# Up projection of a ConvFFN with its weights on the array: channels by tokens instead of tokens by channels

## The chip, the cores and the metric

The kernel runs on one core of a Trainium2 chip. A core has a matrix engine (PE; the loading of its stationary operand has a row of its own, PEld), a vector engine (DVE), a scalar engine (ACT), GpSimd (POOL) and a queue that issues transfers (SP). Matrix products read SBUF and write PSUM, which here is eight banks of 128 by 512 float32. Times are device microseconds of one execution. The program before took 1526.14 us, the median of three runs (1524.74 to 1528.38).

## The reference

One layer of a decoder trunk for 256 tokens of width 2048: a combined projection, two attentions, a gated merge, an output projection, and then a gated feed-forward block with a causal convolution of width 3 over the tokens. Only that last block changes:

```
def conv_ffn(h, w_up, conv_w, conv_b, w_down):
    a, b = jnp.split(h @ w_up, 2, axis=-1)          # h (256, 2048), w_up (2048, 2 x 5632)
    ap = jnp.pad(a, ((0, 0), (CONV_WIDTH - 1, 0), (0, 0)))
    c = conv_b
    for j in range(CONV_WIDTH):
        c = c + conv_w[j] * ap[:, j:j + S]
    return (jax.nn.gelu(c, approximate=True) * b) @ w_down
```

`h` is the RMS-normed residual `x2`. The kernel multiplies the norm's gain into `x2` beforehand; the norm's factor `r` is one number per token, so it can be applied after the product.

## The kernel before

**Products in three parts.** Every float32 operand is held as a rounded high part and the rest as a low part. A product is the sum of high x high, high x low and low x high, three matmuls into one PSUM bank (`mm3`, lines 149 to 151). For weights the split is made on the fly: `wchunk` brings 512 KB of weights (two k-tiles of 128 rows by 512 columns) into a buffer `raw`, ACT copies it rounded to `whi` (L124), DVE subtracts to get `wlo` (L125). There are five `whi`, five `wlo` and three `raw` buffers.

**`gemm`.** For a block of 512 output columns it goes through the k-tiles. The activations are the stationary operand (128 tokens by 128 k), the weights move (512 columns). There are two token tiles, so one k-tile costs six matmuls of 512 columns, and the result stands as tokens by channels in two PSUM banks, one for each token tile.

**The up projection.** `ffn_up(c)` runs for c = 0 to 10, each for 512 channels of the activation half `a` and then the same 512 of the gate half `b`: two `gemm` of eight chunks each. The convolution runs over tokens, so it wants channels by tokens. ACT evacuates each half scaled by `r` (tiles `f`, L866). `conv_cols` then takes 128 channels at a time: four PE transposes (two halves, two token tiles; L844) put `a` and `b` side by side in a PSUM tile `fT`; ACT and DVE do the convolution, the tanh form of the gelu and the product with `b` (L848 to L856); the result is split into `gh` and `gl`, the stationary operand of the down projection.

**What sets the order.** The source hands work to a list of steps: `at(t, f)` puts `f` at a step, and `gemm` calls `tick()` after each chunk. `conv_cols` for the four channel tiles of one c stands at steps 1, 3, 5 and 7 of the next c. A scheduler then sets the order of each engine's queue, and each engine works its queue strictly in that order. The names in the queues carry a running number (`whi_8553`).

**The tiles of activations.** `slot` makes the 16 high and 16 low tiles of each of two sets (`a`, `b`), each 512 numbers wide and holding two k-tiles of 256 tokens. A slot is 520 numbers long (2080 bytes), so that successive slots start at successive multiples of 32 bytes, and `whi`, `wlo` are 1032 numbers long for the same reason.

**The first c** differs: its first `gemm` runs the second token tile's products at the end (`split`), while the residual of that tile is still being computed, and `r` (`rf`) comes from a sum of squares and a Newton iteration on DVE.

Of the kernel before, what the change touches and what calls it, by code (L numbers as in the profile page):

```python
# [23 lines left out]
KT = D // P
# [5 lines left out]
DFF = 5632  # L30
# [11 lines left out]
def trunk_layer(ctx, tc, x, g_mix_pre, g_mix_post, g_ffn_pre, g_ffn_post, w_in, g_q, w_q, g_kv, w_kv,  # L42
                sinks, rel, wo_a, wo_b, w_out, w_up, conv_w, conv_b, w_down, rope_tab, strip_sel, out):
    nc = tc.nc
    vec, act, pe, pool = nc.vector, nc.scalar, nc.tensor, nc.gpsimd
# [6 lines left out]
    pacc = ctx.enter_context(tc.tile_pool(name="pacc", bufs=4, space=PS))  # L52
    pss = ctx.enter_context(tc.tile_pool(name="pss", bufs=2, space=PS))
    pst = ctx.enter_context(tc.tile_pool(name="pst", bufs=2, space=PS))
    dram = ctx.enter_context(tc.tile_pool(name="dram", bufs=1, space=bass.MemoryType.DRAM))
    base = ctx.enter_context(tc.tile_pool(name="base", bufs=1))
    ring = ctx.enter_context(tc.tile_pool(name="ring", bufs=RING))

    def sb(pl, shape, name, dt=F32, tag=None, bufs=None):
        return pl.tile(shape, dt, name=name, tag=tag or name, **({"bufs": bufs} if bufs else {}))  # L60


    ident = sb(base, [P, P], "ident")
# [27 lines left out]


    def slot(name, p, part):
        o = 4 if part == "l" else 0
        return sb(base, [P, 512 + 8], f"{name}{part}{p}", F32R)[:, o:o + 512]

    slot_a = lambda p, part: slot("a", p, part)
    slot_b = lambda p, part: slot("b", p, part)

    def pair_view(tiles):  # L100
        return lambda k: tiles[k // 2][:, (k % 2) * 256:(k % 2) * 256 + 256]
# [4 lines left out]
    def wchunk(src, shape, own=None, rawp=None):  # L106
        i = cnt[0]
        cnt[0] += 1
        n = int(np.prod(shape))
        raw = rawp.tile([P, 1024], F32, name=f"raw{i}", tag="xraw") if rawp else \  # L110
            ring.tile([P, 1024], F32, name=f"raw{i}", tag="raw", bufs=RAW)
        dst = raw[:, :n]
        if len(shape) == 2:
            dst = dst.rearrange("p (a b) -> p a b", a=shape[0])
        elif len(shape) == 3:
            dst = dst.rearrange("p (a b c) -> p a b c", a=shape[0], b=shape[1])
        if len(shape) == 3:
            for k in range(shape[0]):
                nc.sync.dma_start(dst[:, k], src[:, k])
        else:  # L120
            nc.sync.dma_start(dst, src)
        hi, lo = ((own or ring).tile([P, 1024 + (0 if own else 8)], F32R, name=f"w{part}{i}", tag="w" + part)[:, 0:1024]
                  for part in ("hi", "lo"))
        act.copy(hi[:, :n], raw[:, :n])  # L124
        vec.tensor_tensor(lo[:, :n], raw[:, :n], hi[:, :n].bitcast(F32), op=ALU.subtract)  # L125
        return hi, lo
# [3 lines left out]
    now = [0]  # L130

    def at(t, *fs):
        steps[max(t, now[0])].extend(fs)

    def tick():
        for f in steps.pop(now[0], ()):
            f()
        now[0] += 1
# [14 lines left out]
    def gemm(xh, xl, w, k0, nk, c0, n, split=False, pre=None, extra=None):  # L153

        kc = 1024 // n if n in (256, 512) else 2
        acc = new_acc("g")
        todo = []
        cuts = [0, 1, 2] + list(range(4, nk + 1, 2)) if pre else list(range(0, nk, kc)) + [nk]
        for ci, (k, ke) in enumerate(zip(cuts[:-1], cuts[1:])):
            kk = ke - k  # L160
            src = w[(k0 + k) * P:(k0 + k + kk) * P, c0:c0 + n].rearrange("(a p) n -> p a n", p=P)
            if pre and ci == 0:
                pre(k, ke)
            hi, lo = wchunk(src, [kk, n], *(extra or {}).get(ci, ()))
            if pre and ke < nk:
                pre(ke, cuts[ci + 2])
            for j in range(kk):
                kt = k + j
                wh, wl = hi[:, j * n:(j + 1) * n], lo[:, j * n:(j + 1) * n]
                for t in range(NT):  # L170
                    def go(kt=kt, t=t, wh=wh, wl=wl):
                        mm3(acc[t][:, :n], xh(k0 + kt)[:, t * P:(t + 1) * P],
                            xl(k0 + kt)[:, t * P:(t + 1) * P], wh, wl, kt == 0, kt == nk - 1)
                    if split and t == 1:
                        todo.append(go)
                    else:
# [26 lines left out]
    def split_to(hi, lo, src, scale=None):  # L203

        if scale is None:
            act.copy(hi, src)  # L206
            vec.tensor_tensor(lo, src, hi.bitcast(F32), op=ALU.subtract)
        else:
            act.activation(hi, src, AF.Copy, scale=scale)
            vec.scalar_tensor_tensor(lo, src, scale, hi.bitcast(F32), op0=ALU.mult, op1=ALU.subtract)  # L210
# [124 lines left out]
    for g in range(4):  # L335
        at(2 + g, lambda g=g: swa_k(g))

    oth = [slot_b(p, "h") for p in range(8)]
    otl = [slot_b(p, "l") for p in range(8)]
    OH, OL = pair_view(oth), pair_view(otl)  # L340
# [434 lines left out]

    x2h = [slot_b(p, "h") for p in range(8)]
    x2l = [slot_b(p, "l") for p in range(8)]
    HH, HL = pair_view(x2h), pair_view(x2l)
    ssh = [sb(p3, [P, 4], f"ssh{t}") for t in range(NT)]
    rf = [None, None]  # L780

# [20 lines left out]
    def x2_norm(t):  # L802
        for j in range(4):
            act.activation(jk(f"xj{t}_{j}"), x2[t][j], AF.Square, accum_out=ssh[t][:, j:j + 1])
        v = sb(p3, [P, 1], f"vh{t}")
        vec.tensor_reduce(v, ssh[t], axis=AX.X, op=ALU.add)
        vec.tensor_scalar(v, v, 1.0 / D, EPS, op0=ALU.mult, op1=ALU.add)
        r = rsqrt(v, 1, f"rf{t}", p3)
        r2 = sb(p3, [P, 1], f"rfh{t}")
        vec.tensor_scalar(r2, r, 0.5, None, op0=ALU.mult)  # L810
        rf[t] = (r, r2)

    for b in range(4):
        c0, n = W_BLOCKS[b]
# [20 lines left out]
    gT, dsum = [[], []], []  # L835
    GH, GL = pair_view(gT[0]), pair_view(gT[1])

    def conv_cols(sa, k, i, slot):

        w0, w1, w2, cb_ = (cvT[:, 44 * q + k:44 * q + k + 1] for q in range(4))  # L840
        pt = pst.tile([P, 512], F32, name=f"fT{k}", tag="t")
        for q in range(2):
            for t in range(NT):
                pe.transpose(pt[:, q * 256 + t * P:q * 256 + (t + 1) * P], sa[t][q][:, i * P:(i + 1) * P], ident)  # L844
        a, b = pt[:, 0:256], pt[:, 256:512]
        cc = sb(p6, [P, 256], f"cc{k}", tag="cc", bufs=3)
        uu = sb(p6, [P, 256], f"uu{k}", tag="uu", bufs=3)
        act.activation(cc, a, AF.Identity, scale=w2, bias=cb_)  # L848
        vec.scalar_tensor_tensor(cc[:, 1:256], a[:, 0:255], w1, cc[:, 1:256], op0=ALU.mult, op1=ALU.add)
        vec.scalar_tensor_tensor(cc[:, 2:256], a[:, 0:254], w0, cc[:, 2:256], op0=ALU.mult, op1=ALU.add)  # L850
        act.activation(uu, cc, AF.Square)
        vec.tensor_scalar(uu, uu, 0.044715, 1.0, op0=ALU.mult, op1=ALU.add)
        vec.tensor_tensor(uu, uu, cc, op=ALU.mult)
        act.activation(uu, uu, AF.Tanh, scale=GELU_C)
        vec.scalar_tensor_tensor(uu, uu, 1.0, cc, op0=ALU.add, op1=ALU.mult)
        vec.tensor_tensor(uu, uu, b, op=ALU.mult)  # L856
        split_to(GH(slot), GL(slot), uu)

    def ffn_up(c, slot0, first=False):

        sa = [[None, None], [None, None]]

        def evac(acc, q):
            for t in range(NT):
                a = sb(p6, [P, 512], f"f{q}_{c}_{t}", tag="f" + "ab"[q], bufs=4)
                act.activation(a, acc[t], AF.Copy, scale=rf[t][q][:, 0:1])  # L866
                sa[t][q] = a

        acc, todo = gemm(HH, HL, w_up, 0, KT, 512 * c, 512, split=first, extra=first_extra if first else None)
        for f in todo:  # L870
            f()
        if first:
            x2_norm(0)
            x2_norm(1)
        evac(acc, 0)
        if first:
            drain()
            es8.close()
            esx.close()
            es7, p7 = open_pool("p7")  # L880
            for q, part in enumerate("hl"):
                gT[q][:] = [slot_a(i, part) if i < 8 else sb(p7, [P, 512], f"g{part}{i}", F32R) for i in range(12)]
            dsum[:] = [[sb(p7, [P, 512], f"ds{t}_{j}") for j in range(4)] for t in range(NT)]
        acc, _ = gemm(HH, HL, w_up, 0, KT, DFF + 512 * c, 512)
        evac(acc, 1)
        for i in range(4):
            at(now[0] + 1 + 2 * i, lambda i=i: conv_cols(sa, 4 * c + i, i, slot0 + i))
        return es7 if first else None

    es7 = ffn_up(0, 0, first=True)  # L890
# [109 lines left out]
```

## Time and profile before

| | |
|---|---|
| median of three runs | 1526.14 us |
| profiled execution: span | 1523.6 us |
| PE / PEld busy | 99% / 82% of the span |
| DVE / ACT busy | 62% / 52% |
| granted clock of PE, mean | 0.998 |
| transfers | 285 MB, 187 GB/s |

The profile shows one execution. Its own time is given as the span, 1523.6 us from the first to the last instruction; the median of the timed runs is 2.5 us longer, and that difference is taken as what lies around the span. A matmul's row shows its duration from start to end, but matmuls overlap: what one costs is the distance between the starts of two neighbours.

### The profile page before, as it was taken

What the parts mean: (1) busy time and instruction counts of PE and PEld (TensorE: products, weight loads), DVE (VectorE), ACT (ScalarE), POOL (GpSimd) and SP (SyncE); (2) the same over time, 40 slices, a digit from 0 to 9 for tenths busy, and PEclk for the clock granted to TensorE, in tenths of its full rate; (3) what the DMA queues carried; (4) which work ended last, traced back from release to release, by engine and by line L of the source; (5) the groups of instructions that cost most, each with busy time, mean ns of one, the idle gap of its engine ahead of it and who ended that gap; (6) DMA issues with size and microseconds to landing.
All of it is one profiled execution on the core that took longest, in us unless ns stands there. A gap on an engine that the chain in (4) does not pass through costs nothing.

```text
span 1523.6 us, 20149 instructions
## 1 busy us (share of the span) xinstructions
PE 1508.2 (99%) x7347; PEld 1246.6 (82%) x7347; DVE 940.2 (62%) x1607; ACT 799.1 (52%) x1289; POOL 66.8 (4%) x114
## 2 busy tenths in 40 slices
PE   9999999999999999999999999999999999999997
PEld 7888888888899887888888888888888888888887
DVE  5688884444677664655766666666544466666755
ACT  6588874434555553444655545555434455555542
POOL 2122200000000002000000000000000000000000
PEclk9999999999999999999999999999999999999999
DMA  7776666666655658765656666665566666665553
GB/s 236 214 177 166 156 180 188 202 207 201 187 153 153 175 163 298 243 211 186 189 184 179 187 183 181 181 180 181 191 191 186 189 180 180 181 190 181 178 193 113
DMA packets 160803, 285.46 MB, mean 187 GB/s; under 512 B 18419, under 2 KB 33893, under 8 KB 160448
## 3 DMA queue, kind: packets, MB, share of 16 engines
q1 hardware_dynamic: 154736, 264.81, 57.0%
q0 software_dynamic: 5968, 19.36, 5.0%
q8 instruction: 58, 0.95, 0.3%
q14 instruction: 41, 0.34, 0.1%
HBM read 277.79 MB, written 6.34 MB: 186 GB/s over the span
## 4 chain that ended last, share of the span: by engine, by line
PE 93%; DVE 2%; DMA 2%; ACT 2%; issue 1%; SPq 0%; DVEq 0%; ACTq 0%
PE accg L149 28%; PE accg L151 28%; PE accg L150 28%; DMA raw<-in_w_in_dram 1%; PE fT L844 1%; PE mpo L685 1%; DMA raw<-in_w_o_mla_dram 1%; DVE wlo L125 1%; PE ms L651 1%; ACT whi L124 1%; PE qn L616 0%; PE qn L614 0%; PE qn L615 0%; ACT p L411 0%; PE pt L369 0%
## 5 line engine op out<-in xcount | busy, mean ns | idle before, releaser
L125 DVE TENSOR_TENSOR wlo<-raw,whi 128x1024 fp32r<-128x1024 f32 (+2 forms) x501 | 608.8, 1216 | 506.4 <-ACT whi L124 505.7
L124 ACT CAST whi<-raw 128x1024 fp32r<-128x1024 f32 (+2 forms) x501 | 521.5, 1042 | 611.7 <-PE accg L151 514.3
L149 PE MATMUL accg<-whi,bh 128*128 128x512 f32 x960 | 382.3, 398 | 0.0
L151 PE MATMUL accg<-whi,bl 128*128 128x512 f32 x960 | 378.5, 394 | 0.0
L150 PE MATMUL accg<-wlo,bh 128*128 128x512 f32 x960 | 378.1, 394 | 0.0
L149 PE MATMUL accg<-whi,ah 128*128 128x512 f32 (+2 forms) x896 | 347.8, 389 | 0.0
L150 PE MATMUL accg<-wlo,ah 128*128 128x512 f32 (+2 forms) x896 | 344.6, 385 | 0.1
L151 PE MATMUL accg<-whi,al 128*128 128x512 f32 (+2 forms) x896 | 344.0, 384 | 0.0
L151 PEld LDWEIGHTS accg<-whi,bl 128*128 128x128 f32 x960 | 180.2, 188 | 42.6
L150 PEld LDWEIGHTS accg<-wlo,bh 128*128 128x128 f32 x960 | 180.5, 188 | 40.4
L149 PEld LDWEIGHTS accg<-whi,bh 128*128 128x128 f32 x960 | 180.4, 188 | 40.2
L151 PEld LDWEIGHTS accg<-whi,al 128*128 128x128 f32 x896 | 168.6, 188 | 35.0
L150 PEld LDWEIGHTS accg<-wlo,ah 128*128 128x128 f32 x896 | 168.8, 188 | 32.8 <-DVE wlo L125 0.8
L149 PEld LDWEIGHTS accg<-whi,ah 128*128 128x128 f32 x896 | 168.7, 189 | 31.6 <-ACT whi L124 0.2
L149 PE MATMUL accg<-whi,gh 128*128 128x512 f32 (+1 forms) x104 | 39.7, 382 | 0.0
L150 PE MATMUL accg<-wlo,gh 128*128 128x512 f32 (+1 forms) x104 | 39.1, 376 | 0.0
L151 PE MATMUL accg<-whi,gl 128*128 128x512 f32 (+1 forms) x104 | 38.7, 376 | 0.0
L411 ACT ACTIVATE p<-p,nm 128x128 f32<-128x128 f32 x64 | 28.4, 445 | 5.8 <-DVE nm L402 5.8
L844 PEld LDWEIGHTS fT<-ident,f 128*128 128x128 f32 x176 | 21.9, 140 | 6.0
L844 PE MATMUL fT<-ident,f 128*128 128x128 f32 x176 | 26.3, 272 | 0.0
L848 ACT ACTIVATE cc<-fT,cvT 128x256 f32<-128x256 f32 x44 | 24.3, 552 | 0.0
L149 PEld LDWEIGHTS accg<-whi,gh 128*128 128x128 f32 x104 | 19.5, 188 | 4.4 <-ACT gh L206 0.8
(304 smaller groups left out, 1284.9 us busy)
## 6 DMA issues: line engine op xcount, KB each, us to landing
raw<-in_ffn_w_up_dram SPq DMA_DIRECT2D x176, 512.0 KB, 3.9
raw<-in_w_in_dram SPq DMA_DIRECT2D x111, 512.0 KB, 4.3
raw<-in_ffn_w_down_dram SPq DMA_DIRECT2D x88, 512.0 KB, 3.7
raw<-in_w_o_swa_dram SPq DMA_DIRECT2D x32, 512.0 KB, 4.2
raw<-in_w_o_mla_dram SPq DMA_DIRECT2D x32, 512.0 KB, 4.8
raw<-in_w_out_dram SPq DMA_DIRECT2D x32, 512.0 KB, 4.1
raw<-in_mla_w_q_up_dram SPq DMA_DIRECT2D x48, 128.0 KB, 2.7
bias<-strip POOLq DMA_DIRECT2D x16, 256.0 KB, 3.9
```

What stands on the lines that cost most here:

```text
L124: act.copy(hi[:, :n], raw[:, :n])
L125: vec.tensor_tensor(lo[:, :n], raw[:, :n], hi[:, :n].bitcast(F32), op=ALU.subtract)
L149: pe.matmul(o, ah, bh, start=start, stop=False)
L150: pe.matmul(o, ah, bl, start=False, stop=False)
L151: pe.matmul(o, al, bh, start=False, stop=stop)
L411: act.activation(pb[:, i, a:b], pb[:, i, a:b], AF.Exp, bias=st["nm"][:, i, t:t + 1], accum_out=st["sm"][:, i, t:t + 1])
L651: pe.matmul(o, w, v_, start=n == 0, stop=False)
L685: pe.matmul(o, w(t), p_[:, c], start=n == 0, stop=n == 5)
L844: pe.transpose(pt[:, q * 256 + t * P:q * 256 + (t + 1) * P], sa[t][q][:, i * P:(i + 1) * P], ident)
L848: act.activation(cc, a, AF.Identity, scale=w2, bias=cb_)
```

## The change

- **`gemm_t`** is new and computes the up projection, all of it except the `a` half of c = 0. The weights are the stationary operand (128 k by 128 channels), the tokens move. The tokens' high and low parts of one k-tile now lie side by side in one slot of 512 columns (`HS`). For each of four channel tiles, `whi` meets the 512 columns (high and low tokens at once), and `wlo` meets the 256 columns of the high tokens, added to the first half of the same bank. A k-tile of 512 channels is four matmuls of 512 columns and four of 256. Four banks (`pacc`) hold the `a` half, the other four (`pss`, `pst`) the `b` half.
- **The result is already channels by tokens**, so the transposes `fT` go, but for the two of each channel tile in c = 0. In their place ACT copies the low half of the bank to SBUF and DVE adds the high half (`join`), for `a` and for `b`.
- **The factor `r`** can no longer be a per-partition scale. `x2_rows` makes a tile `rfrow` with `r` along the columns (two transposes, once), and DVE multiplies by it, once before the convolution and once after the gelu.
- **The steps:** the convolution of `a` now runs in steps 0 to 3 of the `b` half (`conv_next`), the product with `b` in steps 0 to 3 of the next c (`conv_b`).
- **Lengths:** slots and ring buffers lose their extra 8 numbers, and two pads put the slots and the ring's buffers all at 96 bytes modulo 256.

```
     def slot(name, p, part):
-        o = 4 if part == "l" else 0
-        return sb(base, [P, 512 + 8], f"{name}{part}{p}", F32R)[:, o:o + 512]
+        return sb(base, [P, 512], f"{name}{part}{p}", F32R)
...
+    sb(base, [P, 56], "pad_a")
...
+    def gemm_t(xs, w, nk, c0, acc):
+        for k in range(0, nk, 2):
+            src = w[k * P:(k + 2) * P, c0:c0 + 512].rearrange("(a p) n -> p a n", p=P)
+            hi, lo = wchunk(src, [2, 512])
+            for j in range(2):
+                for i in range(4):
+                    c = j * 512 + i * P
+                    pe.matmul(acc[i], hi[:, c:c + P], xs(k + j), start=k + j == 0, stop=False)
+            for j in range(2):
+                for i in range(4):
+                    c = j * 512 + i * P
+                    pe.matmul(acc[i][:, 0:256], lo[:, c:c + P], xs(k + j)[:, 0:256], start=False, stop=k + j == nk - 1)
+            tick()
...
+    def join(acc, name):
+        a = sb(p6, [P, 512], name, tag="fa", bufs=4)[:, 0:256]
+        act.copy(a, acc[:, 256:512])
+        vec.tensor_tensor(a, a, acc[:, 0:256], op=ALU.add)
+        return a
+
+    def conv_next(acc, k, gs):
+        a = join(acc, f"ca{k}")
+        vec.tensor_tensor(a, a, rfrow[0], op=ALU.mult)
+        conv_a(a, k, gs)
+
+    def conv_b(acc, k, g, slot):
+        b = join(acc, f"cb{k}")
+        vec.scalar_tensor_tensor(g, g, 0.5, b, op0=ALU.mult, op1=ALU.mult)
+        split_to(GH(slot), GL(slot), g)
...
-        acc, _ = gemm(HH, HL, w_up, 0, KT, DFF + 512 * c, 512)
-        evac(acc, 1)
+        else:
+            acc = [pacc.tile([P, 512], F32, name=f"acca{c}_{i}", tag="acc") for i in range(4)]
+            gemm_t(HS, w_up, KT, 512 * c, acc)
+            for i in range(4):
+                at(now[0] + i, lambda i=i: conv_next(acc[i], 4 * c + i, gs))
+        acb = [(pss, pst)[i // 2].tile([P, 512], F32, name=f"accb{c}_{i}", tag="st"[i // 2]) for i in range(4)]
+        gemm_t(HS, w_up, KT, DFF + 512 * c, acb)
         for i in range(4):
-            at(now[0] + 1 + 2 * i, lambda i=i: conv_cols(sa, 4 * c + i, i, slot0 + i))
+            at(now[0] + i, lambda i=i: conv_b(acb[i], 4 * c + i, gg[i], slot0 + i))
```

Two places show how the queues move. The first is PE's queue in the up projection for c = 2. Before, four transposes stand between two chunks of a `gemm` (`accg` is its PSUM tile, `bh` and `bl` are the tokens' high and low parts):

```order
L151 MATMUL accg_0_8172<-whi_8194,bl_6638 128x512
L149 MATMUL accg_1_8173<-whi_8194,bh_6630 128x512
L150 MATMUL accg_1_8173<-wlo_8195,bh_6630 128x512
L151 MATMUL accg_1_8173<-whi_8194,bl_6638 128x512
L844 MATMUL fT_8210<-ident,f_1_0_8018 128x128
L844 MATMUL fT_8210<-ident,f_1_1_8020 128x128
L844 MATMUL fT_8210<-ident,f_1_0_8168 128x128
L844 MATMUL fT_8210<-ident,f_1_1_8170 128x128
L149 MATMUL accg_0_8172<-whi_8230,bh_6631 128x512
```

Now the chunks follow each other with nothing between; this is the end of an `a` half and the first chunk of the `b` half:

```order
L193 MATMUL acca_3_8346<-bl_6646,wlo_8528 128x256
L189 MATMUL accb_0_8547<-bh_6631,whi_8553 128x512
L189 MATMUL accb_1_8548<-bh_6631,whi_8553 128x512
L189 MATMUL accb_2_8549<-bh_6631,whi_8553 128x512
L189 MATMUL accb_3_8550<-bh_6631,whi_8553 128x512
L189 MATMUL accb_0_8547<-bh_6632,whi_8553 128x512
L189 MATMUL accb_1_8548<-bh_6632,whi_8553 128x512
L189 MATMUL accb_2_8549<-bh_6632,whi_8553 128x512
L189 MATMUL accb_3_8550<-bh_6632,whi_8553 128x512
L193 MATMUL accb_0_8547<-bh_6631,wlo_8554 128x256
L193 MATMUL accb_1_8548<-bh_6631,wlo_8554 128x256
```

The transposes are gone, and six matmuls of 512 columns for a k-tile have become four of 512 and four of 256, first all with `whi`, then all with `wlo`.

The second place is DVE's queue. Before, the work of one channel tile is spread over the chunks, with never more than eight other instructions between two `wlo`:

```order
L125 TENSOR_TENSOR wlo_8339<-raw_8336,whi_8338 128x1024
L849 SCALAR_TENSOR_TENSOR cc_8215<-fT_8210,cvT,cc_8215 128x255
L850 SCALAR_TENSOR_TENSOR cc_8215<-fT_8210,cvT,cc_8215 128x254
L125 TENSOR_TENSOR wlo_8357<-raw_8354,whi_8356 128x1024
L852 TENSOR_SCALAR uu_8216<-uu_8216 128x256
L853 TENSOR_TENSOR uu_8216<-uu_8216,cc_8215 128x256
L125 TENSOR_TENSOR wlo_8399<-raw_8396,whi_8398 128x1024
```

Now 22 instructions stand between the fifth and the sixth `wlo` of a `b` half, in every c from 1 to 10. The first ones and the last ones of the 22 for c = 2 (`ca` is the joined `a` of a channel tile, `gg` the gelu's result):

```order
L125 TENSOR_TENSOR wlo_8702<-raw_8699,whi_8701 128x1024
L887 TENSOR_TENSOR ca_8573<-ca_8573,acca_0_8343 128x256
L887 TENSOR_TENSOR ca_8610<-ca_8610,acca_1_8344 128x256
L892 TENSOR_TENSOR ca_8573<-ca_8573,rfrow 128x256
L892 TENSOR_TENSOR ca_8610<-ca_8610,rfrow 128x256
L887 TENSOR_TENSOR ca_8647<-ca_8647,acca_2_8345 128x256
L887 TENSOR_TENSOR ca_8684<-ca_8684,acca_3_8346 128x256
L870 SCALAR_TENSOR_TENSOR cc_8577<-ca_8573,cvT,cc_8577 128x255
```

```order
L876 SCALAR_TENSOR_TENSOR gg_0_8341<-uu_8578,cc_8577 128x256
L874 TENSOR_TENSOR uu_8615<-uu_8615,cc_8614 128x256
L877 TENSOR_TENSOR gg_0_8341<-gg_0_8341,rfrow 128x256
L873 TENSOR_SCALAR uu_8652<-uu_8652 128x256
L892 TENSOR_TENSOR ca_8684<-ca_8684,rfrow 128x256
L874 TENSOR_TENSOR uu_8652<-uu_8652,cc_8651 128x256
L125 TENSOR_TENSOR wlo_8724<-raw_8721,whi_8723 128x1024
```

The convolution of four channel tiles has become one block on DVE, with the tiles' steps interleaved, and the next `wlo` stands behind it. It comes to 22 instructions ahead of the sixth `wlo` and 10 more spread over the next four.

More of the change, by code (lines that the diff above doesn't have):

```diff
@@ L121, in wchunk @@
             nc.sync.dma_start(dst, src)
-        hi, lo = ((own or ring).tile([P, 1024 + (0 if own else 8)], F32R, name=f"w{part}{i}", tag="w" + part)[:, 0:1024]
+        hi, lo = ((own or ring).tile([P, 1024], F32R, name=f"w{part}{i}", tag="w" + part)
                   for part in ("hi", "lo"))
@@ L336, in trunk_layer @@
         at(2 + g, lambda g=g: swa_k(g))
+    sb(base, [P, 8], "pad_b")
     oth = [slot_b(p, "h") for p in range(8)]
@@ L777, in trunk_layer @@
     x2l = [slot_b(p, "l") for p in range(8)]
-    HH, HL = pair_view(x2h), pair_view(x2l)
+    HS = lambda k: (x2h + x2l)[k]
+    HH, HL = (lambda k: HS(k)[:, 0:256]), (lambda k: HS(k)[:, 256:512])
     ssh = [sb(p3, [P, 4], f"ssh{t}") for t in range(NT)]
@@ L808, in x2_norm, with x2_rows @@
         r = rsqrt(v, 1, f"rf{t}", p3)
-        r2 = sb(p3, [P, 1], f"rfh{t}")
-        vec.tensor_scalar(r2, r, 0.5, None, op0=ALU.mult)
-        rf[t] = (r, r2)
+        rf[t] = r
+    def x2_rows():
+        pr = pst.tile([P, 512], F32, name="rfT", tag="t")
+        for t in range(NT):
+            rb = sb(p6, [P, P], f"rfb{t}", tag="uu", bufs=3)
+            vec.tensor_copy(rb, rf[t][:, 0:1].to_broadcast([P, P]))
+            pe.transpose(pr[:, t * P:(t + 1) * P], rb, ident)
+        row = sb(p3, [P, 256], "rfrow")
+        act.copy(row, pr[:, 0:256])
+        return row
     for b in range(4):
@@ L836, in trunk_layer, with conv_a @@
     GH, GL = pair_view(gT[0]), pair_view(gT[1])
-    def conv_cols(sa, k, i, slot):
+    def conv_a(a, k, gs):
         w0, w1, w2, cb_ = (cvT[:, 44 * q + k:44 * q + k + 1] for q in range(4))
[L841 to L845, printed above, removed]
         cc = sb(p6, [P, 256], f"cc{k}", tag="cc", bufs=3)
         uu = sb(p6, [P, 256], f"uu{k}", tag="uu", bufs=3)
+        gg = gs[(k % 4) // 2][:, (k % 2) * 256:(k % 2) * 256 + 256]
         act.activation(cc, a, AF.Identity, scale=w2, bias=cb_)
@@ L854, in conv_cols, with conv_first @@
         act.activation(uu, uu, AF.Tanh, scale=GELU_C)
-        vec.scalar_tensor_tensor(uu, uu, 1.0, cc, op0=ALU.add, op1=ALU.mult)
-        vec.tensor_tensor(uu, uu, b, op=ALU.mult)
-        split_to(GH(slot), GL(slot), uu)
-    def ffn_up(c, slot0, first=False):
[L861 to L871, printed above, removed]
+        vec.scalar_tensor_tensor(gg, uu, 1.0, cc, op0=ALU.add, op1=ALU.mult)
+        vec.tensor_tensor(gg, gg, rfrow[0], op=ALU.mult)
+    def conv_first(sa, k, i, gs):
+        pt = pacc.tile([P, 512], F32, name=f"fT{k}", tag="acc")
+        for t in range(NT):
+            pe.transpose(pt[:, t * P:(t + 1) * P], sa[t][:, i * P:(i + 1) * P], ident)
+        conv_a(pt[:, 0:256], k, gs)
+    def join(acc, name):
[11 more added lines that the diff above has]
+        split_to(GH(slot), GL(slot), g)
+    rfrow = []
+    def ffn_up(c, slot0, first=False):
+        gs = [sb(p6, [P, 512], f"gg{c}_{i}", tag="fb", bufs=4) for i in range(2)]
+        gg = [gs[i // 2][:, (i % 2) * 256:(i % 2) * 256 + 256] for i in range(4)]
         if first:
+            acc, todo = gemm(HH, HL, w_up, 0, KT, 512 * c, 512, split=True, extra=first_extra)
+            for f in todo:
+                f()
             x2_norm(0)
             x2_norm(1)
-        evac(acc, 0)
-        if first:
+            sa = []
+            for t in range(NT):
+                a = sb(p6, [P, 512], f"fa{t}", tag="fa", bufs=4)
+                act.activation(a, acc[t], AF.Copy, scale=rf[t][:, 0:1])
+                sa.append(a)
+            rfrow.append(x2_rows())
             drain()
@@ L883, in ffn_up @@
             dsum[:] = [[sb(p7, [P, 512], f"ds{t}_{j}") for j in range(4)] for t in range(NT)]
-        acc, _ = gemm(HH, HL, w_up, 0, KT, DFF + 512 * c, 512)
-        evac(acc, 1)
+            for i in range(4):
+                at(now[0] + 1 + i, lambda i=i: conv_first(sa, 4 * c + i, i, gs))
+        else:
+            acc = [pacc.tile([P, 512], F32, name=f"acca{c}_{i}", tag="acc") for i in range(4)]
+            gemm_t(HS, w_up, KT, 512 * c, acc)
+            for i in range(4):
+                at(now[0] + i, lambda i=i: conv_next(acc[i], 4 * c + i, gs))
+        acb = [(pss, pst)[i // 2].tile([P, 512], F32, name=f"accb{c}_{i}", tag="st"[i // 2]) for i in range(4)]
+        gemm_t(HS, w_up, KT, DFF + 512 * c, acb)
         for i in range(4):
-            at(now[0] + 1 + 2 * i, lambda i=i: conv_cols(sa, 4 * c + i, i, slot0 + i))
+            at(now[0] + i, lambda i=i: conv_b(acb[i], 4 * c + i, gg[i], slot0 + i))
         return es7 if first else None
```

## The prediction

> **What bounds the kernel now.** I read the page's busy times first, then the chain of waits, then the list of who waited for whom on PE, and last the order of time around one group of transposes.
>
> ```profile
> span 1523.6 us, 20149 instructions
> PE 1508.2 (99%) x7347; PEld 1246.6 (82%) x7347; DVE 940.2 (62%) x1607; ACT 799.1 (52%) x1289; POOL 66.8 (4%) x114
> PE 93%; DVE 2%; DMA 2%; ACT 2%; issue 1%; SPq 0%; DVEq 0%; ACTq 0%
> PE warm L73 <- DVE ident_b L68: 2.0, 1, 2.0
> PE ckT L489 <- DVE ckl L210: 1.3, 1, 1.3
> ```
>
> PE carries 93% of the chain, and its two longest waits on another engine sum to 3.3 us, both far ahead of the feed-forward block. So in that block time is PE's instruction count times the distance of their starts, and nothing else, as long as the weights arrive in time. The distances, in order of time, first around four transposes of c = 1, then in `qn`, an earlier projection that already works the way the change does (weights stationary, 256 token columns moving, a new weight load for each matmul):
>
> ```profile
> 861.44 0.39 PE L151 MATMUL accg<-whi,bl 128*128 128x512 f32 x1
> 861.67 0.60 PE L844 MATMUL fT<-ident,f 128*128 128x128 f32 x4
> 862.02 0.48 PE L149 MATMUL accg<-whi,bh 128*128 128x512 f32 x1
> 862.34 0.39 PE L150 MATMUL accg<-wlo,bh 128*128 128x512 f32 x1
> ...
> 865.11 0.39 PE L150 MATMUL accg<-wlo,bh 128*128 128x512 f32 x1
> 379.27 0.28 PE L614 MATMUL qn<-cqh,whi 128*128 128x256 f32 x1
> ...
> 381.63 0.28 PE L616 MATMUL qn<-cqh,wlo 128*128 128x256 f32 x1
> L844 PE MATMUL fT<-ident,f 128*128 128x128 f32 x176 | 26.3, 272 | 0.0
> ```
>
> A matmul of 512 columns: twelve steps from 862.34 to 865.11 are 2.77 us, 231 ns each. A matmul of 256: the 20 steps from 379.27 to 381.63 are 2.36 us, 118 ns each. Four transposes and the matmul behind them take 861.67 to 862.34, 0.67 us; less one matmul that is 0.44 us for four, 0.11 us each. Nothing hides them: PE is in order and never idle there. Whole chunks show in ACT's casts, which wait for PE to give a buffer back:
>
> ```profile
> 885.45 1.05 ACT L124 CAST whi<-raw 128x1024 fp32r<-128x1024 f32 x1 [1.43 <-PE accg L151]
> 888.28 1.05 ACT L124 CAST whi<-raw 128x1024 fp32r<-128x1024 f32 x1 [1.79 <-PE accg L151]
> 891.08 1.05 ACT L124 CAST whi<-raw 128x1024 fp32r<-128x1024 f32 x1 [1.75 <-PE accg L151]
> 886.53 1.23 DVE L125 TENSOR_TENSOR wlo<-raw,whi 128x1024 fp32r<-128x1024 f32 x1 [1.23 <-ACT whi L124]
> ```
>
> A chunk of twelve matmuls takes 2.80 to 2.83 us here, 2.77 above: 231 to 236 ns a step. I take 232. The cast of a chunk starts when PE frees a buffer, five chunks ahead of its use, and the split ends 2.3 us later (885.45 to 887.76).
>
> **The change part by part.**
>
> *Transposes.* 176 in eleven c become ten (two for each of the four tiles of c = 0, two for `rfrow`). 166 x 0.11 us = 18.3 us off PE, all of it on the path.
>
> *The products.* 21 halves of eight chunks are 168 chunks. A chunk was twelve matmuls of 512; now it is eight of 512 and eight of 256, so the same columns. 8 x 232 + 8 x 118 = 2800 ns against 12 x 232 = 2784: 16 ns more, 2.7 us in all. The price of a step rests on the weight load staying hidden: there are now 16 loads a chunk where there were 12, 672 more in all.
>
> ```profile
> L614 PEld LDWEIGHTS qn<-cqh,whi 128*128 128x128 f32 x64 | 12.1, 188 | 0.0
> ```
>
> A load shows 188 ns, more than the 118 ns step of `qn`, and still the steps hold, so loads overlap matmuls there. Bounds: hidden, nothing more; not hidden at all, 672 x 0.188 = 126 us. I take hidden, since `qn` is the same instruction pair in the same order. [...]
>
> *Alignment.* No view shows addresses, but the slots of before start at eight successive multiples of 32 bytes, so each `gemm` already runs through eight alignments, and its chunks differ by no more than 2.77 to 2.83 us. If one alignment were far better it would show as a shorter chunk. The new program has 4872 matmuls of 512 columns: the 5544 of before (three rows like each of those below), less the 2016 of the 21 halves, plus 1344.
>
> ```profile
> L149 PE MATMUL accg<-whi,bh 128*128 128x512 f32 x960 | 382.3, 398 | 0.0
> L149 PE MATMUL accg<-whi,ah 128*128 128x512 f32 x800 | 319.7, 400 | 0.0
> L149 PE MATMUL accg<-whi,gh 128*128 128x512 f32 x88 | 35.2, 400 | 0.0
> ```
>
> One nanosecond a step is 4.9 us. The rows' spread of chunks (231 to 236) bounds a fixed alignment at -1 to +4 ns, -5 to +19 us; averaged over slots that lie at one alignment each way I take none, and keep 6 us either side as likely.
>
> *ACT and DVE.* They do more, and none of it is priced as long as `wlo` is in time. These rows give the durations (the new 256-column adds and multiplies are taken like L856 and L853):
>
> ```profile
> L848 ACT ACTIVATE cc<-fT,cvT 128x256 f32<-128x256 f32 x44 | 24.3, 552 | 0.0
> L850 DVE SCALAR_TENSOR_TENSOR cc<-fT,cvT,cc 128x254 f32<-128x254 f32 x44 | 21.0, 477 | 0.7
> L849 DVE SCALAR_TENSOR_TENSOR cc<-fT,cvT,cc 128x255 f32<-128x255 f32 x44 | 20.9, 476 | 0.0
> L853 DVE TENSOR_TENSOR uu<-uu,cc 128x256 f32<-128x256 f32 x44 | 18.6, 424 | 1.2
> L855 DVE SCALAR_TENSOR_TENSOR uu<-uu,cc 128x256 f32<-128x256 f32 x44 | 18.5, 419 | 5.0 <-ACT uu L854 5.0
> L856 DVE TENSOR_TENSOR uu<-uu,fT 128x256 f32<-128x256 f32 x44 | 18.2, 414 | 0.7
> L854 ACT ACTIVATE uu<-uu 128x256 f32<-128x256 f32 x44 | 18.1, 412 | 1.7 <-DVE uu L853 1.7
> L206 ACT CAST ah<-uu 128x256 fp32r<-128x256 f32 x32 | 12.9, 403 | 0.0
> L852 DVE TENSOR_SCALAR uu<-uu 128x256 f32<-128x256 f32 x44 | 12.6, 286 | 0.0
> ```
>
> Per c DVE now has 16 splits of 1.22 (19.5 us) and four tiles of eleven instructions, 4.6 us each, together 38 of 44.8 us; before it was 31 of 46.3. It fits, so the danger is only where the work is bunched: the 22 instructions ahead of the sixth `wlo` of a `b` half. Let PE end the `a` half at 0. The fifth chunk's cast and split, freed at that moment, are done at 2.3. The 22 are eight adds and multiplies (3.4), three each of L849 and L850 (2.9), three L852 (0.9), three L853 (1.3) and two of the gelu's end (0.8): 9.2 us, to 11.5 us. Then the split, 1.2: 12.7. PE wants that `wlo` after five chunks of 2.8 and eight matmuls of 0.232, at 15.9. So 3.2 us are spare for DVE's waits on ACT. The next four splits have 5, 1, 2 and 2 instructions ahead, 1.2 + 2.2 us at most, while PE needs 2.8 a chunk, so the lag shrinks from there. Behind the late `wlo` the `raw` buffer frees late too, so its load starts at about 12.7 and lands 3.9 us after, at 16.6, for the chunk that PE reaches at 22.4: in time.
>
> ```profile
> raw<-in_ffn_w_up_dram SPq DMA_DIRECT2D x176, 512.0 KB, 3.9
> ```
>
> *Banks.* At c = 6 the four banks `acca` follow the down projection's two, whose evacuation by ACT and DVE must be awaited for the third and fourth; the same kind of evacuation (L866) takes 0.69 us, against 0.46 us of two matmuls in between. In c = 0 the fourth `accb` bank waits for the copy of `rfT`. I give 0.8 us to both together; zero and 2 us are the ends.
>
> *Sum.* 1523.6 - 18.3 + 2.7 + 0.8 = 1508.8 us of span. With the 2.5 us by which the median of the shown runs exceeds the span, **1511 us**.
>
> **The rivals.**
>
> *DVE comes late and PE waits (slower).* Place: the 22 instructions. If the tiles' work ran one after the other instead of interleaved, each tile's chain would be copy 0.40, add and multiply 0.84, L848 0.55, L849 and L850 0.95, square 0.41, L852 and L853 0.71, tanh 0.41, the gelu's end 0.84: 5.1 us. Three of them behind 2.3, and the split, end at 18.8, 2.9 us too late, ten times: 1511 + 29 = 1540. It costs from 3.2 us of waiting, and the change is a loss from 4.7 us. For it: L855's row shows 5.0 us of idle DVE behind the tanh in 44 tiles, so hand-overs do cost. Against it: that is 0.1 us a tile, and the queue interleaves three tiles.
>
> *The same, only partly (no change).* DVE waits 4.4 to 4.8 us in each block, and PE loses 1.2 to 1.6 us ten times: 1523 to 1527.
>
> *The weight loads are not hidden (slower).* 1511 + 126 = 1637. Only `qn` speaks, and it speaks against.
>
> *The transposes were hidden (it does not do what it says).* Then only the added 3.5 us count: 1530. The 0.67 us between 861.67 and 862.34 speaks against.
>
> *One alignment is better than the mix.* 3 ns a step over 4872 matmuls: 14.6 us more, 1496. The chunks' shortest row, 231 ns, allows one nanosecond only.
>
> **How the numbers follow.** The forecast has 0.73 (1505 to 1517, from the alignment's 6 us), the better alignment 0.09, no change 0.08, DVE late 0.06, loads not hidden 0.02, transposes hidden 0.02. A measurement of this kernel can tell about 0.2%, 3 us, from no change. Faster takes the first two and a little of the third, 0.83; the same 0.07; slower 0.10. The range of 8 in 10 leaves one in ten on each side: 1500 (half of the better alignment) to 1523 (the edge of no change).
>
> **What would show it.** In the profile after: the row of `fT` with 8 transposes; matmuls of 512 in the new line at 231 to 233 ns a step and of 256 at 118; chunks of 2.80 us; the list of PE's waits with nothing over a microsecond from DVE `wlo` in the up projection; one c taking 44.8 us where it took 46.3; DVE at about 67% of the span. Wrong would be: PE waiting for `wlo` about 14 us into each `b` half; steps of 256 columns near 188 ns; or steps of 512 that are all a few nanoseconds off 232, which would be the alignment.

## The result: 1498.9 us, 1.8% less, and 12 us less than the forecast

The changed kernel takes 1498.94 us (median of four runs, 1496.87 to 1502.63), the kernel before 1525.44 beside it: 0.982 of the time, with an interval of 0.981 to 0.984. That is 26.5 us less where 14.8 us less was forecast, and 1 us below the range.

The page of the kernel after (span, busy times, chain of waits), and the list of whom PE waited for:

```profile
span 1496.8 us, 21394 instructions
PE 1479.7 (99%) x7853; PEld 1266.8 (85%) x7853; DVE 988.2 (66%) x1775; ACT 802.3 (54%) x1332; POOL 66.9 (4%) x114
PE 91%; ACT 3%; DMA 2%; DVE 2%; issue 1%; SPq 0%; DVEq 0%; ACTq 0%
```

```profile
PE mT L753 <- DVE lta L772: 2.4, 2, 2.1
PE warm L73 <- DVE ident_b L68: 2.1, 1, 2.1
PE ckT L505 <- DVE ckl L225: 1.8, 1, 1.8
```

PE is still 99% busy, and none of its longest waits lies in the up projection. So the time again is the number of matmuls times the distance of their starts. In order of time, the start of an `a` half, its second chunk, and the start of the `b` half of the same c (`acca` and `accb` are the banks of the two halves):

```profile
888.66 2.00 PE L189 MATMUL acca<-bh,whi 128*128 128x512 f32 x8
890.50 1.12 PE L193 MATMUL acca<-bh,wlo 128*128 128x256 f32 x8
891.46 2.00 PE L189 MATMUL acca<-bh,whi 128*128 128x512 f32 x8
...
911.01 2.00 PE L189 MATMUL accb<-bh,whi 128*128 128x512 f32 x8
```

Eight matmuls of 512 columns take 888.66 to 890.50 (230 ns each), eight of 256 the 0.96 us behind them (120 ns each), and a half of eight chunks 888.66 to 911.01, 22.35 us: 2.794 us a chunk, where the forecast said 2.800. The new work costs what was forecast. The surprise lies in the old `gemm`, which the change doesn't touch. A stretch of the down projection, 57 steps after and 24 steps before:

```profile
1129.62 0.39 PE L151 MATMUL accg<-whi,al 128*128 128x512 f32 x1
...
1142.55 0.39 PE L151 MATMUL accg<-whi,al 128*128 128x512 f32 x1
```

```profile
1137.26 0.40 PE L149 MATMUL accg<-whi,ah 128*128 128x512 f32 x1
...
1142.83 0.40 PE L149 MATMUL accg<-whi,ah 128*128 128x512 f32 x1
```

12.93 us over 57 steps are 226.8 ns; before, 5.57 us over 24 steps were 232.1. Of the old form 3528 matmuls of 512 columns are left (5544 less 2016), and 4 to 5 ns on each are 14 to 18 us, enough for the 12.0 us by which the span (1496.8) lies under the forecast span (1508.8). Two parts of the change could be behind it: the offsets of the tiles, or something that `gemm_t` does to its surroundings.

### The profile page after: what moved, and what is told of

Its sections match the earlier page's. It is cut to its first block, busy times and chain, and to the rows that moved or that the text cites. A ratio compares the mean times of both kernels' runs of the same rounds, so it can differ in the third digit from the quotient of the medians.

```text
span 1496.8 us, 21394 instructions
## 1 busy us (share of the span) xinstructions
PE 1479.7 (99%) x7853; PEld 1266.8 (85%) x7853; DVE 988.2 (66%) x1775; ACT 802.3 (54%) x1332; POOL 66.9 (4%) x114
## 4 chain that ended last, share of the span: by engine, by line
PE 91%; ACT 3%; DMA 2%; DVE 2%; issue 1%; SPq 0%; DVEq 0%; ACTq 0%
PE accg L150 17%; PE accg L149 17%; PE accg L151 17%; PE accb L189 11%; PE acca L189 10%; PE accb L193 6%; PE acca L193 5%; DMA raw<-in_w_o_mla_dram 2%; DMA raw<-in_w_in_dram 1%; ACT whi L124 1%; DVE wlo L125 1%; ACT p L427 1%; PE ms L667 1%; PE mpo L701 1%; PE qn L632 1%
## 5 line engine op out<-in xcount | busy, mean ns | idle before, releaser
L149 PE MATMUL accg<-whi,bh 128*128 128x512 f32 x272 | 107.4, 395 | 0.0
L151 PE MATMUL accg<-whi,bl 128*128 128x512 f32 x272 | 106.8, 393 | 0.0
L150 PE MATMUL accg<-wlo,bh 128*128 128x512 f32 x272 | 106.6, 392 | 0.0
L189 PE MATMUL accb<-bh,whi 128*128 128x512 f32 x352 | 88.6, 393 | 0.0
L189 PE MATMUL accb<-bl,whi 128*128 128x512 f32 x352 | 88.3, 393 | 0.0
L189 PE MATMUL acca<-bh,whi 128*128 128x512 f32 x320 | 80.3, 392 | 0.0
L189 PE MATMUL acca<-bl,whi 128*128 128x512 f32 x320 | 80.1, 392 | 0.0
L189 PEld LDWEIGHTS acca<-bl,whi 128*128 128x128 f32 x320 | 57.5, 189 | 10.3
L151 PEld LDWEIGHTS accg<-whi,bl 128*128 128x128 f32 x272 | 51.4, 189 | 11.0
L150 PEld LDWEIGHTS accg<-wlo,bh 128*128 128x128 f32 x272 | 51.5, 189 | 10.5
L149 PEld LDWEIGHTS accg<-whi,bh 128*128 128x128 f32 x272 | 51.5, 189 | 10.4
```

The costliest lines, as they stand in the source:

```text
L149: pe.matmul(o, ah, bh, start=start, stop=False)
L150: pe.matmul(o, ah, bl, start=False, stop=False)
L151: pe.matmul(o, al, bh, start=False, stop=stop)
L189: pe.matmul(acc[i], hi[:, c:c + P], xs(k + j), start=k + j == 0, stop=False)
```

## The experiments

All ratios are to the kernel before, run on the same chip beside each.

**Each half of the change alone.** The first kernel is before with the new lengths and pads only:

```
     def slot(name, p, part):
-        o = 4 if part == "l" else 0
-        return sb(base, [P, 512 + 8], ...)[:, o:o + 512]
+        return sb(base, [P, 512], ...)
...
+    sb(base, [P, 56], "pad_a")
...
-        hi, lo = (ring.tile([P, 1024 + 8], ...)[:, 0:1024]
+        hi, lo = (ring.tile([P, 1024], ...)
...
+    sb(base, [P, 8], "pad_b")
```

> The kernel before with the slots and the ring's buffers at 96 bytes modulo 256, and nothing else of the change. Theory A, alignment: in the profile after the change, matmuls of 512 columns in the old form step by about 227 ns where they stepped by 232; 5544 such matmuls x 4.5 ns = 25 us less, so about 1500 us. Theory B, the extra gain sits in the new up projection: about 1525 us, steps of 232 ns.

The second is the change with the old lengths and without the pads; `rfrow` moves into a table that is no longer needed, for room:

```
+        o = 4 if part == "l" else 0
+        return sb(base, [P, 512 + 8], ...)[:, o:o + 512]
-    sb(base, [P, 56], "pad_a")
-    sb(base, [P, 8], "pad_b")
-        row = sb(p3, [P, 256], "rfrow")
+        row = rtab.rearrange("p a b c -> p (a b c)")[:, 0:256]
```

> The change with the old lengths and no pads, so that slots and ring buffers lie at successive multiples of 32 bytes as before (rfrow lies in a table that is no longer read, to make room). Theory A: the sum of the prediction without an alignment term, about 1511 us, and old-form steps of 232 ns. Theory B: about 1499 us.

Measured: offsets alone 1503.43 us (1502.67 to 1505.79), ratio 0.986 (0.984 to 0.987); `gemm_t` alone 1511.19 (1510.35 to 1514.70), ratio 0.991 (0.989 to 0.993). The groups of `gemm`'s matmuls with the second slot set, before (two lines; the third stands in the prediction, 382.3 us at 398 ns) and with the offsets alone:

```profile
L151 PE MATMUL accg<-whi,bl 128*128 128x512 f32 x960 | 378.5, 394 | 0.0
L150 PE MATMUL accg<-wlo,bh 128*128 128x512 f32 x960 | 378.1, 394 | 0.0
```

```profile
L149 PE MATMUL accg<-whi,bh 128*128 128x512 f32 x960 | 378.1, 394 | 0.0
L151 PE MATMUL accg<-whi,bl 128*128 128x512 f32 x960 | 374.4, 390 | 0.0
L150 PE MATMUL accg<-wlo,bh 128*128 128x512 f32 x960 | 373.7, 389 | 0.0
```

The same matmuls in the same number are each 4 to 5 ns shorter, in all three lines. And `gemm_t` alone shows both of its parts as forecast. A half, and 24 steps of the down projection:

```profile
895.48 2.02 PE L189 MATMUL acca<-bh,whi 128*128 128x512 f32 x8
...
917.90 2.02 PE L189 MATMUL accb<-bh,whi 128*128 128x512 f32 x8
...
1134.64 0.39 PE L151 MATMUL accg<-whi,al 128*128 128x512 f32 x1
...
1140.20 0.40 PE L151 MATMUL accg<-whi,al 128*128 128x512 f32 x1
```

22.42 us a half (forecast 8 x 2.80 = 22.40), and 231.7 ns a step. Its span is 1508.6 us, against 1508.8 in the prediction's sum. So the sum for the `gemm_t` part was right to 0.2 us, and everything that is missing is the offsets.

The two gains don't add: 22.3 and 14.5 us (each against 1525.70 beside it) are 36.8, and the change has 26.5, 10.3 us less. With equal offsets a half of the old `gemm` would be 96 steps of 227.5 ns (a mean that is explained below), 21.84 us, against 22.35 in `gemm_t`: 0.51 us on each of 21 halves, 10.7 us. At equal offsets the new form is dearer than the old one by that much, not by 2.7 us. The 2.7 us are already in the time of `gemm_t` alone, so 8.0 of the 10.3 us are explained. The spans of the four profiled executions leave 10.7 us, so 2.7 more. In the profile of the change PE waited 2.4 us for `mT`, in those of the two halves 1.4 us each, and right behind that wait its granted clock was 0.50 for 3.4 us (597.7 to 601.1), which loses 1.7: an estimate of 2.7 us. Whether this belongs to the change is not shown; a second profile of it (the run beside the better version below) has 1.5 us for `mT`, and the like drop of the clock in another place (224.8 to 228.2).

**Which offsets count.** First all slots and the ring together 64 bytes on (all at 160 modulo 256), then the ring alone 128 bytes on (slots at 96, ring at 224):

```
-    sb(base, [P, 56], "pad_a")
+    sb(base, [P, 72], "pad_a")
```

> The change with the first pad 64 bytes longer: slots and ring buffers all at 160 modulo 256 instead of 96. If what counts is that moving and stationary operands have the same offset: 1499 us, steps of 227 ns. If 96 itself counts: up to 1511 us.

```
     oth = [slot_b(p, "h") for p in range(8)]
     otl = [slot_b(p, "l") for p in range(8)]
     OH, OL = pair_view(oth), pair_view(otl)
+    sb(base, [P, 32], "pad_c")
```

> The change with 128 bytes between the slots and the ring: slots all at 96, ring buffers all at 224 modulo 256. If both operands must have the same offset: about 1511 us, steps near 232 ns. If it is enough that each kind is at one offset of its own: 1499 us.

Measured: all moved together 1499.38 us (1496.66 to 1499.55), the ratio 0.982 (0.981 to 0.984) that the change has. The ring alone 1512.95 us (1512.34 to 1518.17), ratio 0.992 (0.990 to 0.995): the gain of the offsets is gone. Its half and its 24 steps:

```profile
896.98 2.03 PE L189 MATMUL acca<-bh,whi 128*128 128x512 f32 x8
...
919.46 2.03 PE L189 MATMUL accb<-bh,whi 128*128 128x512 f32 x8
...
1134.73 0.39 PE L149 MATMUL accg<-whi,ah 128*128 128x512 f32 x1
...
1140.34 0.39 PE L149 MATMUL accg<-whi,ah 128*128 128x512 f32 x1
```

22.48 us, and 233.7 ns a step. So 96 is not the point, and neither is that all slots agree among themselves, as they still do here. What counts is how the two operands of a matmul lie to each other.

**Why `gemm_t` gains nothing.** It has two peculiarities: the moving operand stays for four matmuls while the bank changes. In this version of the change each bank takes its two k-tiles one behind the other, so the moving operand alternates:

```
-            for j in range(2):
-                for i in range(4):
+            for i in range(4):
+                for j in range(2):
```

> The change with the two inner loops of gemm_t exchanged: the two k-tiles of a chunk follow each other for one channel tile, so two matmuls in a row write the same bank, and the moving operand changes each time. In the change, steps of 512 columns between two channel tiles are 231 ns in gemm_t, while the old-form steps at the same alignment are 227. If that comes from the moving operand staying the same or from the bank changing at each matmul: steps of 227 ns and 116 ns, 1344 x 3.5 + 1344 x 3 = 9 us less, 1490. If it comes from neither: 1499.

Measured 1497.42 us (1495.67 to 1497.65), ratio 0.981 (0.980 to 0.983), with a half at 22.35 us as in the change (887.67 to 910.02). Changed together, the two leave the half as it was, so they don't explain the difference. The next one moves the second slot set, in which the up projection's tokens lie, 64 bytes up (`rfrow` again in the old table, for room):

```
-    sb(base, [P, 8], "pad_b")
+    sb(base, [P, 24], "pad_b")
...
     OH, OL = pair_view(oth), pair_view(otl)
+    sb(base, [P, 48], "pad_c")
```

> The change with the second set of slots 64 bytes further, at 160 modulo 256, and the first set and the ring at 96. In the run without alignment the gemm_t steps whose next weights lie 64 bytes below the moving tokens (modulo 256) are the shortest: 229 ns for 512 columns and 115 for 256, against 231 and 119 in the change. If this distance decides: 1344 x 1.5 + 1344 x 3.9 = 7.3 us less in gemm_t, and the 816 old-form matmuls that use the second set go from 227 to 233, 4.7 us more: 1496. If equal offsets are best for every form: about 1510.

Measured 1496.69 us (1494.96 to 1498.28), ratio 0.981 (0.980 to 0.983), a half at 22.05 us (890.62 to 912.67). 0.30 us less on each of 21 halves are 6.3 us less; the span is only 2.6 us less, since the set serves other products too, in the old form, and there it is now the stationary operand at an unequal offset.

On average over a run, the steps go by one distance. For each matmul take the start of the next stationary operand less the start of the moving operand, in bytes modulo 256 (addresses from the compiled program; steps from the traces, by setting their starts beside the program's order; the mean over all such pairs of a run):

| distance | 512, old `gemm` | 512, `gemm_t` | 256, `gemm_t` | runs |
|---|---|---|---|---|
| changing | 232.1 ns | about 232 ns | about 118 ns | before, `gemm_t` alone |
| 0 | 227.6 | 230.1 | 119.0 | the change |
| 64 | 233.3 | not seen | not seen | second set moved |
| 128 | 232.7 | 232.8 | 118.6 | ring moved |
| 192 | 228.9 | 229.0 | 115.7 | the change (`gh`); second set moved |
| 224 | not seen | 233.4 | 116.6 | tokens 32 up, below |

In the change the old form's steps at distance 0 fall at 0 modulo 512 with the first slot set and at 256 with the second, 227.9 and 227.3 ns on average, so the table doesn't part the two.

The means hide a second pattern. In the change, at distance 0 throughout, a step of 512 columns in `gemm_t` takes 232.3, 231.2 and 227.7 ns from the first, second and third channel tile to the next, 232.5 from the fourth to the next k-tile, and 226.7 from the fourth to the first matmul with `wlo`. At distance 192 the old form (`gh`) takes 229.2, 231.7 and 225.8 ns on its three lines. So the distance moves the mean, but doesn't set each step; what sets the rest is open.

**A version that beats both.** If the distance moves the mean, only the up projection's tokens should lie 64 bytes up, and every other use of that memory at equal offsets. The second set becomes one tile with two views:

```
-    slot_b = lambda p, part: slot("b", p, part)
+    b_all = []
+    slot_b = lambda p, part, o=0: b_all[0][:, o + 512 * index(p, part):][:, 0:512]
...
+    b_all.append(sb(base, [P, 8192 + 16], "b_all", F32R))
+    sb(base, [P, 48], "pad_c")
...
-    x2h = [slot_b(p, "h") for p in range(8)]
-    x2l = [slot_b(p, "l") for p in range(8)]
+    x2h = [slot_b(p, "h", 16) for p in range(8)]
+    x2l = [slot_b(p, "l", 16) for p in range(8)]
...
+        row = rtab.rearrange("p a b c -> p (a b c)")[:, 0:256]
```

(`index(p, part)` stands for `p + 8 * (part == "l")`.)

> The change with the second slot set as one tile, in which only the up projection's tokens (x2) lie 64 bytes higher, at 160 modulo 256; every other use of the set, the other slots and the ring stay at 96. If what counts is the distance from the moving operand to the next stationary operand modulo 256, the matmuls of gemm_t run at distance 192 at 228.8 and 115.7 ns, as they did when the whole second set was moved (b64), against 230.1 and 118.9 in the change, and the other matmuls of 512 columns stay at 227.5: per chunk 8 x 1.3 + 8 x 3.2 = 36 ns, 168 chunks, 6.0 us less than the change, 1493 (ratio to the kernel before about 0.979). If the step hangs on how many slots share one offset, moving sixteen of them costs: 1499 or more.

And the same with 8 in place of 16, tokens at 128, distance 224:

> The same with x2 32 bytes higher, at 128 modulo 256: distance 224. If the step falls toward 192 in an even way from 0, about half of the 6.0 us, 1496; if 32 bytes are enough to leave distance 0, 1493; if 224 behaves like 64 and 128 (233 ns), 8 x 3 ns a chunk are lost, 4 us: 1503.

Measured: 64 bytes up 1493.77 us (1489.97 to 1495.90), ratio 0.979 (0.977 to 0.981); 32 bytes up 1500.43 (1499.22 to 1500.78), 0.984 (0.982 to 0.985). A chunk and a half of the first, then of the second, and the second's next chunk:

```profile
882.32 2.00 PE L190 MATMUL accb<-b_all,whi 128*128 128x512 f32 x8
884.15 1.07 PE L194 MATMUL accb<-b_all,wlo 128*128 128x256 f32 x8
...
890.57 1.99 PE L190 MATMUL acca<-b_all,whi 128*128 128x512 f32 x8
...
912.62 1.99 PE L190 MATMUL accb<-b_all,whi 128*128 128x512 f32 x8
```

```profile
880.03 2.03 PE L190 MATMUL accb<-b_all,whi 128*128 128x512 f32 x8
881.90 1.09 PE L194 MATMUL accb<-b_all,wlo 128*128 128x256 f32 x8
882.84 2.03 PE L190 MATMUL accb<-b_all,whi 128*128 128x512 f32 x8
```

At distance 192 a half takes 22.05 us (890.57 to 912.62). At 224 eight of 512 take 1.87 us and eight of 256 0.94: the first lose, the second gain, and the sum is a chunk of 2.81. The expected 1503 used 233 ns for the large ones and left out what the small ones gain. Then the change and the better version once more, beside each other:

> The change itself once more, beside the version with x2 64 bytes higher on the same chip. Both theories: 1497 to 1501.

> The version with only x2 64 bytes higher, beside the change on the same chip. If the shorter steps of gemm_t are worth what their sum says, it is 6 us below the change of this call, 1491 to 1495; if the first figure for it was scatter between calls, the two agree within 2 us.

1497.73 us (1496.35 to 1500.01) against 1492.80 (1491.62 to 1494.02). The runs don't overlap; 4.9 us less than the change, ratio to before 0.978 (0.977 to 0.979).

**How near DVE is to being late.** The prediction's largest rival needed 3.2 us of waiting in front of the sixth `wlo` of a `b` half. Two versions lengthen the 22 instructions in that place, by three and by five maxima of a tile with itself for each of four channel tiles, which leave the values as they are:

```
         vec.tensor_tensor(a, a, rfrow[0], op=ALU.mult)
+        for _ in range(3):
+            vec.tensor_tensor(a, a, a, op=ALU.max)
         conv_a(a, k, gs)
```

> The change with three more DVE instructions of 256 columns (the maximum of the joined half with itself, which changes nothing) for each channel tile of c = 1 to 10; 36 instead of 22 instructions stand ahead of the sixth wlo, 14 x 0.34 to 0.42 = 4.8 to 5.9 us. With the 3.2 us to spare of the prediction: 1.6 to 2.7 us late, ten times, 1515 to 1526. With the 5.6 us by which that wlo precedes its first matmul in the profile after the change: at most 0.3 us late, 1499 to 1502.

> The same with five more for each channel tile; 34 to 38 instructions stand ahead of the sixth wlo, and DVE's work for one c is 38 + 20 x 0.38 = 45.6 us against PE's 44.8. If DVE then bounds the up projection: 0.8 us and up for each c, 1507 or more, with PE waiting for wlo. If the overlap of DVE's instructions saves a fifth of their durations: 1499 to 1505.

DVE in the change, in order of time: the fifth split of a `b` half that begins at 911.01, the first and the last of the 22, the sixth split; and PE at the sixth chunk:

```profile
911.34 1.22 DVE L125 TENSOR_TENSOR wlo<-raw,whi 128x1024 fp32r<-128x1024 f32 x1 [1.53 <-ACT whi L124]
912.48 0.74 DVE L887 TENSOR_TENSOR ca<-ca,acca 128x256 f32<-128x256 f32 x2
...
919.64 0.42 DVE L874 TENSOR_TENSOR uu<-uu,cc 128x256 f32<-128x256 f32 x1
919.98 1.22 DVE L125 TENSOR_TENSOR wlo<-raw,whi 128x1024 fp32r<-128x1024 f32 x1
```

```profile
924.98 2.00 PE L189 MATMUL accb<-bl,whi 128*128 128x512 f32 x8
926.82 1.11 PE L193 MATMUL accb<-bl,wlo 128*128 128x256 f32 x8
```

The 22 take 7.5 us (912.48 to 919.98), waits on ACT included, where 9.2 were forecast without any: instructions that follow each other start 0.34 us apart, not the 0.42 of their rows. The sixth `wlo` is done at 921.20 and wanted at 926.82, so 5.6 us were spare, and the same in all ten c. With three more a tile the time is 1524.93 us (1520.38 to 1529.60), ratio 1.000 (0.999 to 1.001), with five 1542.15 (two runs), 1.011. PE's wait is there, on the line and tile that the prediction named, in the first and in the second version:

```profile
PE accb L193 <- DVE wlo L125: 18.4, 8, 3.1
```

```profile
PE accb L193 <- DVE wlo L125: 29.7, 9, 5.7
```

The waits sum to 18.4 and 29.7 us, but the times are 26.0 and 43.2 us above the change. The rest is in part the clock. One of the waits of the second version, and what follows it:

```profile
886.19 2.07 PE L193 MATMUL accb<-bl,wlo 128*128 128x256 f32 x8 [3.38 <-DVE wlo L125]
888.06 3.62 PE L189 MATMUL accb<-bl,whi 128*128 128x512 f32 x8
891.48 1.27 PE L193 MATMUL accb<-bl,wlo 128*128 128x256 f32 x8
```

Eight matmuls of 512 columns take 888.06 to 891.48 here, 427 ns each, and the granted clock is 0.50 from 885.0 to 891.8. The mean clock of the second version is 0.988, of the change 0.997: 0.009 of 1541 us are 14 us, about the 13.5 that the waits leave. For the first (0.995) it is 3 of 7.6 us, and the rest is not accounted for. A wait of PE can thus cost more than its own length.

In the first version 36 instructions stand ahead of the sixth `wlo`, 14 more, since the scheduler put two others there too; at 0.34 us they are 4.8 us, less than the 5.6 spare, so by the spare time alone nothing should have been lost. The same place with three more, in a `b` half that begins at 915.66:

```profile
920.09 1.23 DVE L125 TENSOR_TENSOR wlo<-raw,whi 128x1024 fp32r<-128x1024 f32 x1 [1.31 <-ACT whi L124]
921.23 0.75 DVE L887 TENSOR_TENSOR ca<-ca,acca 128x256 f32<-128x256 f32 x2
...
933.34 1.22 DVE L125 TENSOR_TENSOR wlo<-raw,whi 128x1024 fp32r<-128x1024 f32 x1
```

```profile
919.00 1.05 ACT L124 CAST whi<-raw 128x1024 fp32r<-128x1024 f32 x1 [1.48 <-DMA raw<-in_ffn_w_up_dram]
```

```profile
934.61 1.21 PE L193 MATMUL accb<-bl,wlo 128*128 128x256 f32 x8 [2.97 <-DVE wlo L125]
```

The stretch grew by 4.6 us (12.1 against 7.5), but it also began late: the fifth split ended 5.7 us after the half's start (921.32), in the change 1.55 (912.56). ACT's cast had waited for the raw weights, not for PE: splits that run late free the raw buffers late, their loads land late, and the lead of the splits no longer recovers from one c to the next. The trace bears this out. In c = 1 and c = 6, which no long stretch precedes, the fifth split ends 1.55 us after the half's start, as in the change, and the sixth `wlo` is 1.0 us early; in the other eight c the fifth split ends 3.9 to 5.8 us after the start and PE waits. So my two theories for this run were both wrong: 1524.9 us lies in the range of the first, 3.2 us to spare, but its spare time is refuted by the 5.6 measured; the second counted the spare time rightly and took it for granted that it is the same in each c. For five more, 1542 us lies in the open range of the first theory (1507 or more), with PE waiting for `wlo`, but DVE doesn't bound the up projection as that theory had it: in the `b` half that begins at 866.8 and the `a` half behind it DVE is busy for 41.2 of 50.9 us.

## Why the prediction was right or wrong

**Right: transposes, products, banks.** The groups of transposes, and of the new small weight loads, in the change:

```profile
L881 PE MATMUL fT<-ident,fa x8: 270/272/274, 781.6 to 790.8; 128*128 128x128 f32 x8
L833 PE MATMUL rfT<-ident,rfb x2: 272/272/273, 775.7 to 775.8; 128*128 128x128 f32 x2
```

```profile
L193 PEld LDWEIGHTS accb<-bl,wlo 128*128 128x128 f32 x352 | 48.0, 190 | 3.5
L189 PEld LDWEIGHTS accb<-bh,whi 128*128 128x128 f32 x352 | 63.2, 189 | 11.6 <-ACT rfrow L835 0.3
L189 PEld LDWEIGHTS acca<-bh,whi 128*128 128x128 f32 x320 | 57.5, 189 | 10.6 <-DVE ds L952 0.3
```

Ten are left of 176. `gemm_t` alone gave the sum -18.3 + 2.7 + 0.8 to 0.2 us; the two waits for banks that 0.8 us were given for show 0.3 us each. One c takes 44.7 us (two halves of 22.35), forecast 44.8. The loads stay hidden: steps of 120 ns under loads of 190. With the 672 added loads on the path the time was to be 1637 us; it was 1498.94. What lets a load and running matmuls overlap, no run here shows.

**Right in its verdict, wrong in its size: ACT and DVE.** No wait for `wlo`, but with 5.6 us to spare, not 3.2: the durations of the rows overlap by 0.08 us from one DVE instruction to the next, 1.7 us over the 22, and the fifth split ended 0.75 us earlier than the 2.3 us put down for it. Missed was the coupling through the raw buffers ("in time", the prediction said of the next load), which makes a stretch of DVE that is too long cost more than its own excess: with three more a tile PE waited 18.4 us in all, where the spare time alone left nothing to wait for.

**Wrong: alignment.** The step that failed reads "If one alignment were far better it would show as a shorter chunk", with the conclusion "averaged over slots that lie at one alignment each way I take none". The eight alignments of before are those of one operand. What moves the mean step is the distance between two operands, and in before both sides walk, slots and ring, each by 32 bytes a tile, with the low slots another 16 off. No chunk of before had twelve steps at one distance, so a shorter chunk could not show. Nor do single pairs: those that happen to lie at distance 0 in before (434 of the old form) take 231.6 ns on average, barely less than the 232.1 of all. In these runs the 227.5 ns come only where neighbours lie at distance 0 too; why a lone pair has less of it is open.

The term was set at 0 with -5 to +19 us as its ends; it measured -12 (1496.8 against 1508.8). The gain sits in the 3528 matmuls that the change leaves as they were. The rival "One alignment is better than the mix" named the mechanism, and 1496, with a chance of 0.09; it spread 3 ns over 4872 matmuls, while it is 4 to 5 ns on 3528 and next to nothing on those of `gemm_t`. The text had also named the sign that would refute it, "steps of 512 that are all a few nanoseconds off 232, which would be the alignment", and that is what came. A row that bears only on a mixture should have bound the mixture, not each of its parts: the honest range for a fixed alignment was wider than the spread of chunks that all hold the same mix.

**Open.** Why distance 0 gives `gemm_t` 230 and 119 ns where the old form has 227.5 and 192 gives it 229 and 116, is not settled; the order of the banks and the moving operand that stays, exchanged together, made no difference. Where all tiles keep fixed offsets, the weights in use and the next ones lie at the same distance from the moving operand, so these runs don't tell which of the two counts. Nor do they show what in the chip the distance acts on.

## What to carry to other kernels

Where PE is the bound, read the distance of starts of its matmuls, and if it isn't the same in all products, try where the stationary and the moving operand start modulo 256 bytes: here equal starts were best for the old form, and weights 64 bytes below the tokens were better for `gemm_t`. In this kernel pads of a few hundred bytes gave 22 us of 1525, more than the rewritten product. Two gains that were each measured alone may not be added where one makes cheaper what the other takes away. And the time that an engine has to spare is measured in the queue, from the end of the late thing to the start of its reader, for more than one round, since what it delays (here the loads into three raw buffers) may take the spare time of the next round. A wait of PE is to be priced with the slower clock that may come with it, as in the run with five more maxima, where the granted clock was 0.50 for 6.8 us in and after a wait of 3.38 us.

## What the runs showed of the hardware that was not expected

A matmul of 512 float32 columns takes on average between 227.5 and 233.4 ns from start to start, and within one form of product the mean moves with where the tiles start, at nearly the same clock (0.997 to 0.999). The order isn't even: 0 and 192 are short (in the old form 227.6, 228.9), 64, 128 and 224 long (233.3, 232.7, in `gemm_t` 233.4), and for 256 columns 192 is shortest (115.7) and 0 longest (119.0). In the old form that is up to 2.5% of a step of 512 columns (227.6 against 233.3 ns), and what changes the mean is where the stationary operand lies relative to the moving one: when the ring alone was moved, it went from 227.6 to 232.7 ns. What in the chip makes the difference, no row shows.
